# Sums of a weight matrix with ten and seven staging tiles, six column tiles on the first scale, and score tables scaled three steps behind their loads

## The chip, the cores and the metric

The kernel runs on one core of a Trainium2 chip. A core has a matrix engine (PE, TensorE), a vector engine (DVE), an activation engine (ACT), a general engine (POOL, GpSimd) and a queue that issues transfers (SP). Each engine takes its instructions strictly in the order of the program and they meet at semaphores. Working memory is SBUF (128 partitions); PE writes into the eight banks of PSUM.

The metric is the device time of one execution in microseconds. Before the change three runs took 531.81, 538.27 and 540.64 us; the median is 538.27 us.

## The reference, cut to what matters

One encoder block: a combined projection of x (1024 tokens, 1024 features), two groups of attention heads, a gate, an output projection, a residual and a layer norm.

```python
h = x @ W_in                                   # 1024 x 3328 columns
q_a, k_a, v_a, z_a, q_b, k_b, v_b, z_b = split(h)
# group A: 8 heads, 2-D neighbourhood (8 rows x 16 columns of a 16 x 64 grid)
s = einsum(q_a, gathered k_a) * 64**-0.5 + rel_bias       # a table per head and query
y_a = softmax(s) @ gathered v_a
# group B: 8 query heads on 2 key heads, |i - j| <= 128, rotary, a sink logit per head
s = einsum(rotary(q_b), rotary(k_b)) * 64**-0.5           # masked to the band
y_b = softmax(concat(s, sink))[..., :-1] @ v_b
mixed = concat(y_a * silu(z_a), y_b * silu(z_b))
x = layer_norm(2**0.25 * x + mixed @ W_out, gain, bias)
```

## The kernel before, in words

**Numbers.** Most products are computed from 16-bit parts: a matrix is scaled by a power of two and split into a high and a low half, and each product is three matmuls (high by high, high by low, low by high). The value projection uses 32-bit parts instead, so it needs no scale and comes first.

**Scales.** x has one scale, from its largest magnitude. The columns of W_in other than the values' are cut into 21 column tiles of 128 columns (`ORDER`: zb0, z0, zb1, kb, qb0, z1, ...), each in two halves `m` of 512 rows, so there are 42 halves. A scale for the weights comes from sums of magnitudes: `scan_load` (L383) brings a half into a staging tile, `scan` (L388) has ACT sum its magnitudes along each partition. The sums of the first `NG0` column tiles give one scale, those of the others a second one. `chain(i, ...)` (L390 to L403) turns a set of maxima or sums into a scale: a reduction on DVE, a transpose on PE (L394), a second reduction, and some small steps. Chain 0 is x's scale, chain 1 the first weight scale, chain 2 the second.

**The early part** is written out by hand. The value projection (L366) runs in 16 banks, eight for the first half of the tokens and eight for the second. During the second half ACT makes the first sums, and x is loaded a second time (`x2_load`, L411) and split into 16-bit halves (`x16_part`, L421 to L426; on ACT, and on DVE or POOL). ACT copies each bank out (`v_out`, L434), DVE keeps running maxima of the values (`v_max`, L441 and L442). The staging tiles of sums and of x have one tag, `xr`, with four buffers. A weight half for a product is loaded by `w_load` (L146), its high part made on ACT (L157), its low part on POOL in two steps (L162, L163).

After that a planner orders the instructions, by its own estimates: the projections of the first column tiles (`pump_all`, matmuls at L296), the remaining sums, and the values: they are scaled, cast to two 16-bit halves in tiles `vt` with three buffers (L544, L545), stored to a scratch array `vd` (L547) and rearranged from there (L551). The SiLU of the first three gate tiles is taken right from the bank (L262).

**The main loop** is in a hand-written order again. It runs over 128 units (64 of group B, 64 of group A), a unit being 128 queries of a head. In step i: `stage_load` for unit i + `LD`; `stage_qk` (scores, L639 and L640 on PE; the minimum of table plus scores on DVE, L647); `stage_tr` for the unit before (the probabilities are split into halves by ACT, L673, and DVE, L674, and a transposing transfer on SP turns them, L677); `stage_pv` four units at a time (L702); `stage_exp` (L663). Between them `pump_to` puts 48 matmuls of the next column tile, at a set pace. Other work waits in a queue for each engine: `enq` puts an operation in, `pop` takes those whose dependencies were put out in an earlier step, at most so many a step, lowest `prio` first; `need` takes one at once. An operation for SP has a lag of two more steps.

**The score tables** of group A (the bias in a dense layout) are loaded by `stage_load` (L612) into tag `bs` with `BR` = 3 buffers, three tables for eight units, and multiplied in place by a scale on POOL (L614). Before the change that operation has no dependency in its queue and the highest priority, so it is put out in the step of its load.

Of the kernel before, what the change touches and what calls it, by code (L numbers as in the profile page):

```python
# [7 lines left out]
F32 = mybir.dt.float32  # L8
# [11 lines left out]
KT = D // 128  # L20
# [30 lines left out]
def hybrid_block(ctx, tc, xT, x, wt, wv, wo, bias, sink, gain, lbias, cos, sin, bmask, out):  # L51
    nc = tc.nc
# [39 lines left out]
    sg = const.tile([128, 2], F32, name="sg")  # L92
# [48 lines left out]
    NH = 2 * len(ORDER)  # L141
# [176 lines left out]
    with ExitStack() as vctx:  # L318
# [55 lines left out]
        def x_max(half, k):  # L374
            i = 8 * half + k
            nc.vector.tensor_reduce(xm[:, i:i + 1], xh[half, k].bitcast(F32), axis=AXX, op=ALU.max,
                                    apply_absolute_value=True)

        scans = {}

        def scan_load(m):
            scans[m] = vp.tile([128, 512], F32, tag="xr", name="wscan", bufs=4)
            nc.sync.dma_start(scans[m], wt[m // 2, m % 2].rearrange("p k c -> p (k c)"))  # L383

        def scan(m):
# [21 lines left out]

        def x2_load(j):
            if j < len(x2):
                x2raw[j] = vp.tile([128, 512], F32, tag="xr", name="xraw2", bufs=4)  # L410
                nc.sync.dma_start(x2raw[j], xT[x2[j]])  # L411

        def x16_part(j):
# [33 lines left out]
        with tc.manual_schedule():  # L447
            first = load_wv(0, (0, 320, 640)), load_x(0, 0, (0, 256, 512))
            for i in (0, 1, 1):
                next(first[i])  # L450
            interleave(*first)
            interleave(load_wv(1), load_x(0, 1))
            for k in range(KT):
                if k + 2 < KT:
                    interleave(load_wv(k + 2), load_x(0, k + 2))
                if k >= X1AT:
                    interleave(load_x(1, 2 * (k - X1AT)))
                    interleave(load_x(1, 2 * (k - X1AT) + 1))
                    x_max(0, k - X1AT)
                for ps in ([0], [1], [2]) if k == 0 else ([0, 1, 2],):  # L460
                    for a in range(2):
                        for t in range(4):
                            v_mms(banks[2 * t + a], t, a, k, ps)
            nc.sync.dma_start(bm, bmask)
            nc.sync.dma_start(sk, sink)
            for m in range(4):
                scan_load(m)
            for i in range(8):
                v_out(banks[i], i // 2, i % 2)
            for k in range(4, KT):  # L470
                x_max(0, k)
            for k in range(KT):
                x_max(1, k)
            for i in range(8):
                ps = bank(tags[i])
                for k in range(KT):
                    v_mms(ps, 4 + i // 2, i % 2, k)
                v_out(ps, 4 + i // 2, i % 2)
                if i < 2:
                    for m in range(4 * i, 4 * i + 4):  # L480
                        scan(m)
                        if i == 0:
                            scan_load(m + 4)
                        else:
                            x2_load(m - 4)
                if i == 1:
                    chain(0, xm, "ot")
                if 2 <= i < 6:
                    for j in range(4 * (i - 2), 4 * (i - 2) + 4):
                        x16_part(j)  # L490
                        x2_load(j + 4)
                if i == 2:
                    for m in range(4):
                        w_load(m)
                if i == 3:
                    chain(1, wm[0], "ot")
                if i == 4:
                    w_split(0)
                    w_split(1)
                if i == 5:  # L500
                    for nm, src, tag in (("cos", cos, "zc"), ("sin", sin, "zs")):
                        tiles[nm] = zslot(nm, tag)
                        nc.sync.dma_start(tiles[nm], src)
                    nc.vector.tensor_scalar_mul(nsk, sk, -1.0)
                if i > 1:
                    v_max(3)

        for m in range(2 * NG0, 2 * NG0 + 4):
            scan_load(m)
        pump_all(["zb0"])  # L510
        for m in range(2 * NG0, NH):
            scan(m)
            if m + 4 < NH:
                scan_load(m + 4)
# [71 lines left out]
    sns = [ap.tile([128, 388], F32, name=f"sn{i}", bufs=1) for i in range(2)]  # L586
    for t in split:
        nc.gpsimd.memset(t, 0.0)
    LD = 4
    bulk = {"last": None, "step": None}  # L590
    st = {}
    on = {}
# [7 lines left out]
        lo, hi = max(t - 1, 0), min(t + 2, 8)  # L600
        return 128 * (hi - lo), [128] * (hi - lo)

    def stage_load(u):
        g, p, j, t, _ = u
        n, _c = geom(u)
        if g == "a":
            b, half = t
            if half == 0 and b != 2:
                bulk["last"] = clock["step"] + 1
                bt = ap.tile([128, 2, 384], F32, tag="bs", name="bias", bufs=BR)  # L610
                o = 2 * BOFF[b]
                nc.sync.dma_start(bt[:, :, :n], bias[2 * p + j, :, o:o + 2 * n].rearrange("p (h n) -> p h n", h=2))  # L612
                bv = bt[:, :, :n]
                op = enq("pool", lambda: nc.gpsimd.tensor_scalar(bv, bv, rsg, -1.0, op0=ALU.mult, op1=ALU.mult),  # L614
                         prio=0)
                st["bias"] = bt, op
            st[u, "b"] = st["bias"][0][:, half, :n], st["bias"][1]

    def stage_qk(u):
# [27 lines left out]
        nc.vector.tensor_tensor_reduce(sn[:, :n], ps[:, :n], bias_t, sg[:, c:c + 1], init,  # L647
                                       op0=ALU.add, op1=ALU.min, accum_out=nm)
        st[u, "sn"] = sn
# [89 lines left out]
    nc.vector.reciprocal(rsg, sg[:, 1:2])  # L739
# [347 lines left out]
```

## Time and profile before

| what | value |
|---|---|
| runs, median (lowest to highest) | 538.27 us (531.81 to 540.64) |
| the profiled execution | 535.45 us, span 533.7 us |
| PE, DVE, ACT, POOL busy | 87%, 67%, 56%, 41% of the span |
| mean granted PE clock | 0.95 |
| moved by the 16 DMA engines | 89.97 MB, 169 GB/s |

The profile shows one execution. "Busy" counts instructions at work, not waits. A window row gives, for a stretch of time, the busy time of each engine with its instructions in brackets, then the granted clock of PE (1.00 is full speed), the mean busy share of the DMA engines, and GB/s. A wait row names the engine and line that waited, what came last before it could go on, and the total, the count and the longest in us. A timeline row gives start, duration, engine, line, output and input; in square brackets stands the idle time of the engine before it and what ended it. "The chain" is the chain of work that ended last, followed back from the last instruction.

### The profile page before, as it was taken

The numbers are of one execution on the slowest core, as the hardware profiler recorded it, in microseconds if no ns is written. First come the engines' busy times: TensorE is split into PE (matmuls) and PEld (weight loads), VectorE is DVE, ScalarE is ACT, GpSimd is POOL, SyncE is SP. The second block draws the span as 40 slices with busy tenths as digits, with TensorE's granted clock in tenths as the row PEclk, the third lists the DMA queues.
The fourth block names the chain that finished last, engine by engine and source line by source line (L and its number), as shares of the span: only waits on it lengthen the run. The fifth ranks groups of instructions, "written<-read, shape, count | busy, mean of one in ns | idle before, by whom it ended". The sixth has DMA issues, their size and how long they took to land.

```text
span 533.7 us, 9570 instructions
## 1 busy us (share of the span) xinstructions
PE 466.1 (87%) x3243; PEld 302.3 (57%) x3243; DVE 359.5 (67%) x823; ACT 296.5 (56%) x701; POOL 220.9 (41%) x231
## 2 busy tenths in 40 slices
PE   8997697796599999899997839599788999999994
PEld 6996673332244555455554424255444568888883
DVE  5874696537277888889885834476485774929834
ACT  4636256796148787777775734466485764402201
POOL 0003192268634725666214444622346443505331
PEclk9999699989699999999999987799799999999998
DMA  7837557898615676677897878787997898364311
GB/s 252 254 102 215 181 152 281 269 293 286 197 39 102 117 135 137 104 140 118 148 181 187 168 122 184 159 152 160 204 210 127 174 190 248 118 242 133 142 60 60
DMA packets 140737, 89.97 MB, mean 169 GB/s; under 512 B 102032, under 2 KB 118416, under 8 KB 140432
## 3 DMA queue, kind: packets, MB, share of 16 engines
q1 hardware_dynamic: 140544, 89.21, 68.2%
q8 instruction: 25, 0.41, 0.4%
q14 instruction: 24, 0.20, 0.1%
q10 hardware_dynamic: 144, 0.15, 0.1%
HBM read 58.92 MB, written 9.96 MB: 129 GB/s over the span
## 4 chain that ended last, share of the span: by engine, by line
PE 60%; DMA 11%; issue 8%; DVE 7%; ACT 7%; POOL 6%; SPq 1%; POOLq 0%; ACTq 0%; DVEq 0%
PE ps_pj L296 25%; PE ps_s L828 6%; PE ps_t L702 5%; PE ps_t L828 4%; PE ps_pj L828 4%; DMA wscan<-in_wt 4%; DMA bias<-in_bias 3%; PE ps_pj L366 3%; ACT wscan L388 3%; POOL wl L163 3%; PE ps_s L639 3%; PE ps_t L366 3%; PE ps_s L640 2%; PE ps_ot L828 2%; PE ps_s L366 2%
## 5 line engine op out<-in xcount | busy, mean ns | idle before, releaser
L296 PE MATMUL ps_pj<-xf,wh 128*128 128x512 f16 x672 | 207.3, 388 | 8.9 <-ACT wh L157 5.5
L296 PE MATMUL ps_pj<-xf,wl 128*128 128x512 f16 x336 | 130.2, 389 | 29.1 <-POOL wl L163 29.1
L296 PEld LDWEIGHTS <-wh 128*128 128x128 f16 x672 | 64.8, 99 | 73.5 <-issue 9.3
L663 ACT ACTIVATE ps_s<-sn,nm 128x385 f32<-128x385 f32 (+3 forms) x128 | 70.3, 549 | 63.9 <-DVE nm L647 62.8
L674 DVE SCALAR_TENSOR_TENSOR split<-ps_s,split 128x384 f16<-128x384 f32 (+2 forms) x128 | 65.6, 513 | 28.0 <-ACT split L673 27.2
L296 PEld LDWEIGHTS <-wl 128*128 128x128 f16 x336 | 33.5, 100 | 72.5 <-POOL wl L163 34.2
L673 ACT ACTIVATE split<-ps_s 128x384 f16<-128x384 f32 (+2 forms) x128 | 57.5, 449 | 18.4 <-DMA tr<-split 16.6
L162 POOL TENSOR_SCALAR wr<-wr,sc 128x512 f32<-128x512 f32 x42 | 34.1, 812 | 67.6 <-ACT wh L157 50.6
L647 DVE CUSTOM_DVE_ANT_0 sn<-ps_s,bias,sg 128x288 f32<-128x288 f32 (+1 forms) x64 | 36.1, 565 | 37.5 <-PE ps_s L640 30.2
L614 POOL TENSOR_SCALAR bias<-bias,rsg 128x576 f32<-128x576 f32 (+1 forms) x24 | 19.2, 798 | 90.6 <-DMA bias<-in_bias 63.0
L163 POOL TENSOR_TENSOR wl<-wr,wh 128x512 f16<-128x512 f32 x42 | 49.7, 1185 | 3.2
L647 DVE CUSTOM_DVE_ANT_0 sn<-ps_s,bm,nsk 128x384 f32<-128x384 f32 (+1 forms) x64 | 40.8, 638 | 8.9 <-PE ps_s L640 8.3
L639 PE MATMUL ps_s<-ks,qs 128*128 128x384 f16 (+2 forms) x128 | 40.2, 314 | 6.0 <-DVE split L674 4.7
L702 PEld LDWEIGHTS <-tr 128*128 128x128 f16 (+1 forms) x1104 | 38.4, 100 | 7.3 <-DMA tr<-split 5.3
L640 PE MATMUL ps_s<-ks,qs 128*128 128x384 f16 (+2 forms) x128 | 40.2, 314 | 0.0
L157 ACT ACTIVATE wh<-wr,sc 128x512 f16<-128x512 f32 x42 | 29.4, 709 | 11.9 <-PE ps_pj L296 11.9
L388 ACT ACTIVATE wscan<-wscan 128x512 f32<-128x512 f32 x42 | 26.2, 625 | 13.7 <-DMA wscan<-in_wt 13.5
L828 PE MATMUL ps_s<-wo,m 128*128 128x512 f32 (+1 forms) x144 | 32.5, 374 | 0.0
L883 ACT ACTIVATE sd<-mv,eps 128x1 f32<-128x1 f32 x8 | 2.4, 295 | 51.8 <-DVE mv L881 51.8
L423 POOL TENSOR_SCALAR xraw<-xraw,sc 128x512 f32<-128x512 f32 x6 | 5.6, 930 | 58.5 <-ACT xf L421 58.5
L828 PE MATMUL ps_pj<-wo,m 128*128 128x512 f32 (+1 forms) x120 | 28.9, 377 | 0.4 <-POOL m L811 0.4
L220 POOL COPY ks<-ks 64x512 f16<-64x512 f16 x40 | 25.4, 647 | 6.9 <-DVE ks L190 3.5
(148 smaller groups left out, 864.4 us busy)
## 6 DMA issues: line engine op xcount, KB each, us to landing
wscan<-in_wt SPq DMA_DIRECT2D x42, 256.0 KB, 3.6
wr<-in_wt SPq DMA_DIRECT2D x42, 256.0 KB, 3.0
xraw<-in_xT SPq DMA_DIRECT2D x31, 256.0 KB, 3.2
bias<-in_bias SPq DMA_DIRECT2D x16, 288.0 KB, 3.4
wor<-in_wo SPq DMA_DIRECT2D x16, 256.0 KB, 4.6
xr<-in_x SPq DMA_DIRECT2D x8, 512.0 KB, 6.3
out<-xr SPq DMA_DIRECT2D x14, 256.0 KB, 2.1
bias<-in_bias SPq DMA_DIRECT2D x8, 384.0 KB, 3.7
```

Source lines behind the costliest of these rows:

```text
L163: nc.gpsimd.tensor_sub(l, raw, h)
L296: nc.tensor.matmul(ps, a[:, k % 4, :], mv, start=(k == 0 and i == 0), stop=(k == KT - 1 and i == 2))
L366: nc.tensor.matmul(ps[:, :320], lh[t // 4, k][:, ts], rh[k][:, cs], start=(k == 0 and i == 0), stop=(k == KT - 1 and i == 2))
L388: nc.scalar.activation(t, t, AF.Abs, accum_out=wm[g][:, i:i + 1])
L639: nc.tensor.matmul(ps[:, :n], q, sl[0], start=True, stop=False)
L640: nc.tensor.matmul(ps[:, :n], q, sl[1], start=False, stop=True)
L647: nc.vector.tensor_tensor_reduce(sn[:, :n], ps[:, :n], bias_t, sg[:, c:c + 1], init, op0=ALU.add, op1=ALU.min, accum_out=nm)
L663: nc.scalar.activation(pt[:, :m], sn[:, :m], AF.Exp, bias=nm, scale=-1.0, accum_out=sm[:, k:k + 1])
L673: nc.scalar.activation(hl[:, :m, 0, :c], src, AF.Copy, scale=PSCALE)
L674: nc.vector.scalar_tensor_tensor(hl[:, :m, 1, :c], src, PSCALE, hl[:, :m, 0, :c], op0=ALU.mult, op1=ALU.subtract)
L702: nc.tensor.matmul(ps[:, HD * m:HD * m + HD], a, b_, start=(i == 0), stop=(i == len(mms) - 1))
L828: nc.tensor.matmul(ps, lh[:, ts], rh[:, cs], start=(e == EO[0] and i == 0), stop=(e == EO[-1] and i == 2))
```

## The change

It has two parts. In the early part:

- `NG0` goes from 4 to 6: the sums of the first six column tiles (12 halves in place of 8) give the first weight scale, and 30 halves remain for the second.
- The staging tiles of the sums and of the second load of x come from `stage`, which goes round ten buffers: the four of `xr`, three of `wvr` (used for the value weights until then) and three of `vt`; from the 31st on it goes round seven, without `vt`. Ten loads are put out ahead in place of four.
- Chains 0 and 1 stand inside the second and third bank of the second half (after the fifth of their eight parts), in place of after the second and the fourth bank.
- The remaining sums stand, in the program, behind the values' casts and the projections of z0 and zb1; four projections and then chain 2 follow in the order kb, qb0, chain 2, z1. The planner still orders all this.
- Scores of the first B heads are scaled by the first scale twice, so there is a third column in `sg`.

In the main loop: `LD` is 5 in place of 4, `BR` is 4 in place of 3, and the scaling of a table gets a dependency that stands for its load (with SP's lag), so it is put out three steps after it.

```diff
-LTT, LPP, BP, BH, BR, ND, NA, NX, F1 = 1, 5, 2, 7, 3, 1, 1, 6, 0.2
+LTT, LPP, BP, BH, BR, ND, NA, NX, F1 = 1, 5, 2, 7, 4, 1, 1, 6, 0.2
-NG0 = 4
+NG0 = 6
...
-        scans = {}
+        scans, staged = {}, [0]
+
+        def stage(name):
+            tag = ("xr", "xr", "xr", "xr", "wvr", "wvr", "wvr", "vt", "vt", "vt")[staged[0] % (10 if staged[0] < 30 else 7)]
+            staged[0] += 1
+            if tag == "xr":
+                return vp.tile([128, 512], F32, tag="xr", name=name, bufs=4)
+            return vp.tile([128, 640], F32, tag=tag, name=name, bufs=3)[:, :512]
 
         def scan_load(m):
-            scans[m] = vp.tile([128, 512], F32, tag="xr", name="wscan", bufs=4)
+            scans[m] = stage("wscan")
...
-            for m in range(4):
+            for m in range(10):
                 scan_load(m)
...
+            nxt = [10]
+
+            def scan_more(n):
+                for m in n:
+                    scan(m)
+                    if nxt[0] < 2 * NG0:
+                        scan_load(nxt[0])
+                    else:
+                        x2_load(nxt[0] - 2 * NG0)
+                    nxt[0] += 1
+
+            scan_more(range(6))
             for i in range(8):
-                ps = bank(tags[i])
-                for k in range(KT):
-                    v_mms(ps, 4 + i // 2, i % 2, k)
-                v_out(ps, 4 + i // 2, i % 2)
-                if i < 2:
-                    for m in range(4 * i, 4 * i + 4):
-                        scan(m)
...
-                if i == 1:
-                    chain(0, xm, "ot")
...
-                if i == 3:
-                    chain(1, wm[0], "ot")
...
                 if i > 1:
-                    v_max(3)
-
-        for m in range(2 * NG0, 2 * NG0 + 4):
-            scan_load(m)
+                    v_max(2)
+                ps = bank(tags[i])
+                for k in range(KT):
+                    v_mms(ps, 4 + i // 2, i % 2, k)
+                    if i in (1, 2) and k == 4:
+                        chain(i - 1, xm if i == 1 else wm[0], "ot")
+                v_out(ps, 4 + i // 2, i % 2)
+                if i == 0:
+                    scan_more(range(6, 2 * NG0))
+            v_max(16)
+
         pump_all(["zb0"])
-        for m in range(2 * NG0, NH):
-            scan(m)
-            if m + 4 < NH:
-                scan_load(m + 4)
...
+        pump_all(ORDER[1:3])
+        nxt = [2 * NG0]
+        for m in range(2 * NG0, NH):
+            if m < 2 * NG0 + 7:
+                scan_load(m)
+        for m in range(2 * NG0, NH):
+            scan(m)
+            if m + 7 < NH:
+                scan_load(m + 7)
...
-    LD = 4
+    LD = 5
...
-    def stage_load(u):
+    def stage_load(u, i):
...
+                ld = Op("sp", None, [], 1)
+                ld.step = i
                 op = enq("pool", lambda: nc.gpsimd.tensor_scalar(bv, bv, rsg, -1.0, op0=ALU.mult, op1=ALU.mult),
-                         prio=0)
+                         ld, prio=0)
...
-        c = 0 if g == "b" else 1
+        c = min(p, 1) if g == "b" else 2
...
-    pump_all(ORDER[1:NG0 - 1])
+    pump_all(ORDER[3:NG0 - 1])
     chain(2, wm[1], "ot")
...
-    for c in range(2):
-        nc.vector.tensor_scalar(sg[:, c:c + 1], inv[:, c, 0:1], inv[:, 1, 0:1], -0.125 / QSCALE ** 2,
+    for c, (i, j) in enumerate(((0, 0), (0, 1), (1, 1))):
+        nc.vector.tensor_scalar(sg[:, c:c + 1], inv[:, i, 0:1], inv[:, j, 0:1], -0.125 / QSCALE ** 2,
                                 op0=ALU.mult, op1=ALU.mult)
...
-                stage_load(units[i + LD])
+                stage_load(units[i + LD], i)
```

More of the change, by code (lines that the diff above doesn't have):

```diff
@@ L91, in hybrid_block @@
     inv = const.tile([128, 2, 2], F32, name="inv")
-    sg = const.tile([128, 2], F32, name="sg")
+    sg = const.tile([128, 3], F32, name="sg")
     rsg = const.tile([128, 1], F32, name="rsg")
@@ L409, in x2_load @@
             if j < len(x2):
-                x2raw[j] = vp.tile([128, 512], F32, tag="xr", name="xraw2", bufs=4)
+                x2raw[j] = stage("xraw2")
                 nc.sync.dma_start(x2raw[j], xT[x2[j]])
@@ L473, in hybrid_block @@
                 x_max(1, k)
-            for i in range(8):
-                ps = bank(tags[i])
-                for k in range(KT):
-                    v_mms(ps, 4 + i // 2, i % 2, k)
-                v_out(ps, 4 + i // 2, i % 2)
-                if i < 2:
-                    for m in range(4 * i, 4 * i + 4):
-                        scan(m)
-                        if i == 0:
-                            scan_load(m + 4)
-                        else:
-                            x2_load(m - 4)
-                if i == 1:
-                    chain(0, xm, "ot")
+            nxt = [10]
[8 more added lines that the diff above has]
+            scan_more(range(6))
+            for i in range(8):
                 if 2 <= i < 6:
@@ L490, in hybrid_block @@
                         x16_part(j)
-                        x2_load(j + 4)
+                        x2_load(nxt[0] - 2 * NG0)
+                        nxt[0] += 1
                 if i == 2:
@@ L505, in hybrid_block @@
                 if i > 1:
-                    v_max(3)
-        for m in range(2 * NG0, 2 * NG0 + 4):
-            scan_load(m)
+                    v_max(2)
[8 more added lines that the diff above has]
+            v_max(16)
         pump_all(["zb0"])
-        for m in range(2 * NG0, NH):
-            scan(m)
-            if m + 4 < NH:
-                scan_load(m + 4)
         cm = vw.tile([128, 5], F32, name="cm")
@@ L731, in stage_ot @@
                 nc.vector.scalar_tensor_tensor(z, src, z_col(p), z, op0=ALU.mult, op1=ALU.mult)
-    pump_all(ORDER[1:NG0 - 1])
+    pump_all(ORDER[3:NG0 - 1])
     chain(2, wm[1], "ot")
     nc.vector.tensor_scalar(vscb, vsc, inv[:, 1, 1:2], None, op0=ALU.mult)
-    for c in range(2):
-        nc.vector.tensor_scalar(sg[:, c:c + 1], inv[:, c, 0:1], inv[:, 1, 0:1], -0.125 / QSCALE ** 2,
+    for c, (i, j) in enumerate(((0, 0), (0, 1), (1, 1))):
+        nc.vector.tensor_scalar(sg[:, c:c + 1], inv[:, i, 0:1], inv[:, j, 0:1], -0.125 / QSCALE ** 2,
                                 op0=ALU.mult, op1=ALU.mult)
-    nc.vector.reciprocal(rsg, sg[:, 1:2])
+    nc.vector.reciprocal(rsg, sg[:, 2:3])
     pump_all(ORDER[NG0 - 1:NPRO])
```

## The prediction

> **What bounds the kernel now.** The page's busy times come first, then the span cut into its stages, then the waits of each stage.
>
> ```profile
> PE 466.1 (87%) x3243; PEld 302.3 (57%) x3243; DVE 359.5 (67%) x823; ACT 296.5 (56%) x701; POOL 220.9 (41%) x231
> ...
> core 0: us, PE busy (x) PEld busy (x) DVE busy (x) ACT busy (x) POOL busy (x), PEclk, DMA share, GB/s
> 35.40:75.20 39.80, 31.22 (x196) 30.84 (x195) 24.44 (x44) 21.54 (x46) 14.97 (x14) 0.87 0.51 159
> 75.20:161.00 85.80, 68.24 (x301) 29.78 (x301) 48.95 (x90) 47.73 (x108) 43.92 (x47) 0.92 0.70 224
> 161.00:281.30 120.30, 116.70 (x988) 64.89 (x987) 104.38 (x275) 93.50 (x235) 57.24 (x55) 1.00 0.73 134
> 281.30:436.70 155.40, 127.84 (x1095) 72.69 (x1094) 96.47 (x263) 93.55 (x243) 72.41 (x87) 0.92 0.83 170
> 436.70:533.70 97.00, 88.33 (x473) 72.92 (x471) 59.17 (x113) 22.40 (x43) 31.70 (x25) 0.97 0.45 141
> ```
>
> The window rows are stages: second half of the value projection; the first six column tiles (zb0 to z1); the 64 units of group B; the 64 units of group A; the output. PE is the bound in the third: 116.7 of 120.3 us busy at full clock. It isn't in the first, second and fourth, where it idles 8.6, 17.6 and 27.6 us and also loses clock. What it waits for there (from 30 to 140 us, then from 280 to 440 us, then POOL and the load queue):
>
> ```profile
> PE ps_pj L296 <- POOL wl L163: 10.0, 2, 8.1
> PE ps_ot L394 <- DVE gm L392: 8.6, 1, 8.6
> PE ps_pj L296 <- ACT wh L157: 3.6, 2, 2.1
> PE ps_pj L296 <- ACT z L262: 3.4, 3, 2.2
> ...
> PE ps_pj L296 <- POOL wl L163: 18.4, 7, 4.9
> PE ps_t L702 <- DMA tr<-split: 4.3, 6, 1.6
> PE ps_s L639 <- DVE split L674: 3.1, 3, 1.2
> ...
> POOL bias L614 <- DMA bias<-in_bias: 63.0, 15, 10.4
> ...
> SPq L383 <- ACT wscan L388: 30.9, 27, 10.6
> ```
>
> The columns are us in total, times, longest. Two things stand out. Early, PE waits for scales (the chains at L394) and for the weight parts that need them; the sums under those scales are fed by loads that wait for four buffers to come free (30.9 us). Late, PE waits for low weight parts (wl) that POOL makes late, because POOL stands in front of a score table whose load has just been issued.
>
> **The change, part by part.**
>
> *Group A: tables loaded five units ahead, scaled three steps later, one more buffer.* From the chain, the timelines of SP and POOL, and the landing times of the table loads (least, median, most):
>
> ```profile
> 346.70 1.50 PE ps_t L702 x36
> 349.82 1.29 PE ps_pj L296 x6
> 362.33 1.05 PE ps_t L702 x36
> ...
> 352.28 0.57 SPq L612 DMA_DIRECT2D bias<-in_bias  x1
> 356.33 0.90 POOL L614 TENSOR_SCALAR bias<-bias,rsg 128x768 f32<-128x768 f32 x1 [8.21 <-DVE nm L647]
> 357.98 1.16 POOL L163 TENSOR_TENSOR wl<-wr,wh 128x512 f16<-128x512 f32 x1
> ...
> DMA to landing us min/median/max: 3.1/3.5/5.3
> ```
>
> From 346.70 to 362.33 PE never waits: two quads, eight units, 15.63 us, so 1.954 us a unit; 64 units are 125.1 us. The stage takes 155.4, so 30.3 us are stalls and halved clock. The rows at 352 to 358 show the mechanism: the table is asked for at 352.28, the scaling at the head of POOL's queue can't start before 356.33, and wl starts only behind it. (The row names DVE; the landing row says 3.5 us is ordinary for the load.) The next weight load on SP waits for that wl, and the transposes of the probabilities queue behind the load, so one late wl costs two engines.
>
> In the changed kernel the scaling is put into POOL's queue three steps after the load: 3 x 1.95 = 5.9 us, longer than the slowest landing (5.3), and the use is two steps (3.9 us) later. So POOL finds its table there and the 63.0 us of waiting go; what was behind it starts when its own input is ready. All 24 scalings stay, 0.9 us each as in the row above or less, and POOL has room (72.4 of 155.4 us busy). What is late next: the waits for tr and split, 7.4 us together, partly effects of the same blocked queue. I leave 5 us of them; the bounds are 0 and 15. **Term: -25 us, between -30 and -15.** That the 161 to 281 us stage runs PE 97% busy with a like load of ACT and DVE speaks for it. The fourth buffer and the earlier load add 3 KB per partition and no instruction; the loads keep their number and pass one transpose more on SP.
>
> *Twelve sums in the first group, ten staging tiles, chains one bank earlier.* From the chain, the timelines of ACT, DVE and PE, and two windows:
>
> ```profile
> 35.44 7.05 PE ps_pj L366 x48
> ...
> 36.06 0.50 ACT L434 COPY v<-ps_ot 128x320 f32<-128x320 f32 x1
> 39.31 0.63 ACT L388 ACTIVATE wscan<-wscan 128x512 f32<-128x512 f32 x1
> 39.94 0.62 ACT L388 ACTIVATE wscan<-wscan 128x512 f32<-128x512 f32 x1
> ...
> 50.67 0.48 DVE L441 SCALAR_TENSOR_TENSOR vmax<-v,vmax 128x320 f32<-128x320 f32 x1
> 55.13 2.96 DVE L426 SCALAR_TENSOR_TENSOR xf<-xraw,sc,xf 128x512 f16<-128x512 f32 x3
> ...
> 58.21 0.47 PE L394 MATMUL ps_ot<-identf,gm 128*128 128x128 f32 x1 [8.58 <-DVE gm L392]
> ...
> 54.00:58.00 4.00, 0.00 (x0) 0.00 (x0) 3.96 (x5) 1.44 (x3) 1.95 (x2) 0.50 0.86 308
> 60.00:64.00 4.00, 4.00 (x17) 4.00 (x16) 2.68 (x7) 0.00 (x0) 0.00 (x0) 0.50 0.45 144
> ```
>
> A sum is 0.62 us on ACT. Now the transpose of the first weight chain stands on PE after the fourth of eight banks and waits 8.6 us, since its reduction on DVE is queued behind conversions of x. In the changed order it stands inside the third bank, at about 44.9 us (35.4 + 2 banks + five eighths of one, at 7.05/2 = 3.5 us, + a transpose). ACT does six sums from 36.6, a copy, six more: until 44.4; a copy; then the first conversions, from 44.8. DVE has ahead of the reduction two low halves of x (the second when ACT has made its third, 46.8 to 47.5) and two pairs of maxima; three pairs took 50.67 to 55.13, 1.5 us a pair. So the reduction is at about 50.5, the transpose at 50.7: PE waits 5.8 us in place of 8.6, with the rest of its third bank and five more behind it. The clock row: after 8.6 us idle it was 0.50 until 64, with 6 us of work under it, 3 us lost. I keep 2.6 of it. The stage then ends at 50.7 + 1.3 + 5 x 3.5 + 2.6 = 72.1 in place of 75.2. **Term: -3, between 0 and -6.**
>
> The Trainium skill has a rule on this loss: TensorE: Matmul & The Clock Gate, Part 1, The HAM clock gate, says the array drops to half rate after a window of about 3.4 us idle and returns after one busy window of the same length. The trace agrees that 8.6 us idle brings 0.50 and it shows up to three such windows. By the rule 5.8 us idle would cost one or two half-rate windows, 1.7 to 3.4 us: an estimate from that page, against the 2.6 taken.
>
> *The first six tiles on the first scale; the other 30 sums behind them.* From the timelines of ACT, DVE and PE, and the landing times of the value stores:
>
> ```profile
> 105.07 0.71 ACT L544 CAST vt<-v 128x640 f16<-128x640 f32 x1
> 122.10 0.72 ACT L544 CAST vt<-v 128x640 f16<-128x640 f32 x1
> 124.18 0.19 DVE L392 TENSOR_REDUCE gm<-wm 128x1 f32<-128x34 f32 x1 [0.43 <-ACT wscan L388]
> 139.52 0.61 PE L296 MATMUL ps_pj<-xf,wl 128*128 128x512 f16 x1 [8.11 <-POOL wl L163]
> 160.97 0.27 PE L639 MATMUL ps_s<-ks,qs 128*128 128x256 f16 x1
> ...
> DMA to landing us min/median/max: 2.8/4.0/4.4
> ```
>
> Six tiles are 288 matmuls of 1.29/6 = 0.215 us: 62 us, 63.5 with the ten small transposes and the first scores. The stage takes 85.8, so 22.3 us are excess: waits of 17.6 and halved clock. The 8.1 us wait goes: the parts of tiles five and six no longer need the second scale (chain 2, whose reduction ran at 124.18), they need the first, which is there at 52 (50.7 and the chain's small steps). The 3.4 for the SiLU evacuations mostly goes: ten, then seven staging tiles let sums run ahead, so the evacuation doesn't stand behind a sum waiting for its load. Some of the 3.6 us for wh stays.
>
> What is new: ACT's order puts all eight casts of the values ahead of the third tile's second evacuation (zb1's SiLU) and ahead of the last two sums. The casts have three tiles, each free only once its store has landed (4.0 us, the last row), so they go in three rounds: my walk through the order puts the first at 96 us, the rounds at 105 and 111, that evacuation at 113. PE has done kb's first 14 matmuls by 108 and waits for the bank: 5 us. The last two loads on SP stand behind the stores and land at 117; the chain's transpose, at 120 on PE, finds its input. So the excess left is 5, plus 2 for wh, wl and clock: 7. **Term: -15.3, between -22 (no excess) and -4 (the casts take their 17 us from 105 as now and the evacuation comes at 123).**
>
> The extra scale column is one DVE operation, hidden: DVE is busy 49 of 85.8 us there. Same sums, same bytes.
>
> *Unchanged:* group B (PE bound) and the output, 97 us.
>
> **Sum.** 25 + 3 + 15.3 = 43.3. The profiled execution took 535.45 us (span 533.7): 535.45 - 43.3 = 492. The median of the runs, 538.27 (531.81 to 540.64), is 0.5% above it; I don't add that, as it is inside their spread. I predict 491.
>
> **The rivals.**
>
> 1. *Transfers become group A's bound.* A window inside the stage, and the packets of the stage:
>
> ```profile
> 350.00:360.00 10.00, 10.00 (x85) 5.70 (x83) 8.75 (x26) 7.15 (x20) 2.73 (x3) 1.00 0.99 182
> DMA packets 63640, 26.47 MB, mean 169 GB/s; under 512 B 51719, under 2 KB 60935, under 8 KB 63623
> ```
>
> The stage's share of 0.83 over 155.4 us is 129 us of transfer time; at 125 us it would be over 1. Against it: the 350 row has 0.99 at full PE pace. If transfers hold the stage at 0.92, it takes 140: gain 15, 502 us. Chance 0.15. The Trainium skill, DMA: Bandwidth & Descriptors, Specifications, asks for 512 B or more per transfer for full rate; that most packets here are under it agrees with a near-full share at 182 GB/s, and by that rule this rival is the outcome.
>
> 2. *The last two sums and the casts keep the early stage as long as now.* It keeps all but 4 of its excess: 535.45 - 25 - 3 - 4 = 503. Chance 0.13.
>
> 3. *The table change doesn't do what it says*: wl is late for ACT's sake and not for the table's. For it: some scalings' rows name DVE or ACT as releaser. Against it: 63.0 us name the load. Group A unchanged: 517. Chance 0.08.
>
> 4. *Slower: scaled tables come late.* POOL works in order, and the scaling is now placed behind other work, 2 units before use. It decides from a lateness over 3.9 us. Then scores wait on DVE and PE, 24 times; if each costs 2.7 us, 65 us are lost, and with the early gain of 18 and the old stalls gone (-25) the time is 557. Against it: POOL is busy 47% there. Chance 0.04.
>
> **How the numbers follow.** Forecast 491, chance 0.52; all terms at their best, about 478: 0.08. The range takes the forecast, rivals 1 and 2 and most of the good end: 477 to 512. Two per cent (about what measurements of this kernel can tell from no change) would be 527 to 549; only rival 4 and a coincidence of 2 and 3 (528) come near. Faster 0.92, same 0.04, slower 0.04.
>
> **What would show it.** The profile after: POOL's wait for the table near zero and PE's wait for wl after 280 us under 4; group A near 130 us; PE's chain wait near 6 us at 45 to 51; unit 0's scores about 18 to 25 us earlier; a wait of PE for zb1's evacuation at 108 to 113. It is wrong if DMA share in group A is over 0.95 with long tr waits, if the casts run past 120, or if DVE waits for tables.

## The result, and the profile after

The changed kernel takes 491.93 us, the median of four runs (490.97 to 494.27), against 536.57 us of the kernel before in the same comparison: a ratio of 0.920, interval 0.912 to 0.928. The forecast was 491. The profiled execution took 492.28 us, its span is 490.5.

The page's busy times of the changed kernel, and its five stages (start, end, length, busy time of each engine, granted clock of PE, DMA share, GB/s):

```profile
PE 456.6 (93%) x3243; PEld 299.3 (61%) x3243; DVE 360.5 (74%) x824; ACT 295.9 (60%) x701; POOL 225.6 (46%) x231
...
35.40:72.80 37.40, 30.77 (x193) 30.39 (x191) 25.45 (x41) 25.79 (x65) 18.52 (x17) 0.86 0.66 209
72.80:147.40 74.60, 66.56 (x305) 29.85 (x303) 48.92 (x94) 44.09 (x95) 43.77 (x43) 0.98 0.66 213
147.40:267.00 119.60, 116.75 (x1003) 65.25 (x1003) 102.98 (x273) 91.75 (x233) 60.63 (x60) 1.00 0.75 138
267.00:394.50 127.50, 121.27 (x1088) 70.42 (x1084) 97.23 (x265) 94.48 (x243) 70.52 (x84) 0.99 1.03 208
394.50:490.50 96.00, 87.21 (x466) 71.80 (x464) 58.74 (x108) 21.47 (x40) 31.45 (x24) 0.98 0.42 142
```

The same work on PE, in less time: its busy share rises from 87% to 93%. Stage by stage, before and after (the second stage ends about where z1's matmuls end; in the changed kernel the scores of unit 0 stand inside it, at 138.7 us against 161.0 before):

| stage | before | after | difference | forecast |
|---|---|---|---|---|
| value projection, second half | 39.8 | 37.4 | -2.4 | -3 |
| first six column tiles | 85.8 | 74.6 | -11.2 | -15.3 |
| group B | 120.3 | 119.6 | -0.7 | 0 |
| group A | 155.4 | 127.5 | -27.9 | -25 |
| output | 97.0 | 96.0 | -1.0 | 0 |
| sum | | | -43.2 | -43.3 |

The sum is right partly because errors cancel, which is luck: the six tiles gave 4.1 us less than forecast, group A 2.9 more and the output 1.0. The 491 also rests on taking the profiled 535.45 us as the start; from the median of 538.27 the same sum gives 495.

What PE still waits for, from 30 to 140 us and then from 240 to 400 us (total, times, longest):

```profile
PE ps_ot L401 <- DVE gm L399: 6.6, 1, 6.6
PE ps_pj L296 <- ACT z L262: 3.6, 1, 3.6
PE ps_pj L296 <- POOL wl L163: 3.1, 2, 1.8
...
PE ps_pj L296 <- ACT wh L157: 2.4, 1, 2.4
PE ps_pj L296 <- POOL wl L163: 1.7, 2, 1.5
PE ps_t L722 <- DMA tr<-split: 1.6, 3, 0.8
```

The wait of 8.1 us for the second scale is gone, and the 18.4 us for wl in group A are down to 1.7. The two that the forecast named as new or left are there: the first weight chain (6.6), and zb1's evacuation (3.6).

The next rows are from the waits in group A: POOL in the changed kernel, then SP in the kernel before, where it stood with a load of w until POOL had made wl.

```profile
POOL bias L634 <- DMA bias<-in_bias: 27.7, 11, 5.1
```

```profile
SPq L146 <- POOL wl L163: 23.8, 8, 5.0
```

POOL's wait for tables is halved, not gone. The row of SP, 23.8 us before, has no counterpart in the changed kernel: no load of w waits for POOL in group A any more.

### The profile page after: what moved, and what is told of

It reads as the page before. It is cut to its first block, busy times and chain, and to the rows that moved or that the text cites. A ratio compares the mean times of both kernels' runs of the same rounds, so it can differ in the third digit from the quotient of the medians.

```text
span 490.5 us, 9560 instructions
## 1 busy us (share of the span) xinstructions
PE 456.6 (93%) x3243; PEld 299.3 (61%) x3243; DVE 360.5 (74%) x824; ACT 295.9 (60%) x701; POOL 225.6 (46%) x231
## 4 chain that ended last, share of the span: by engine, by line
PE 50%; DMA 14%; DVE 11%; issue 10%; ACT 6%; POOL 6%; SPq 3%; POOLq 0%; ACTq 0%; DVEq 0%
PE ps_pj L296 25%; PE ps_t L722 5%; DMA wscan<-in_wt 4%; PE ps_s L848 4%; PE ps_pj L848 4%; DMA xraw<-in_xT 4%; PE ps_t L848 3%; PE ps_s L659 3%; PE ps_s L660 3%; DMA tr<-split 2%; POOL wl L163 2%; POOL wr L162 2%; PE ps_ot L848 2%; DMA wor<-in_wo 1%; PE ps_ot L742 1%
## 5 line engine op out<-in xcount | busy, mean ns | idle before, releaser
L296 PE MATMUL ps_pj<-xf,wh 128*128 128x512 f16 x672 | 203.8, 382 | 6.4 <-ACT z L262 3.6
L296 PE MATMUL ps_pj<-xf,wl 128*128 128x512 f16 x336 | 127.9, 381 | 5.3 <-POOL wl L163 5.3
L659 PE MATMUL ps_s<-ks,qs 128*128 128x384 f16 (+2 forms) x128 | 39.8, 311 | 4.2 <-DVE split L694 1.9
L660 PE MATMUL ps_s<-ks,qs 128*128 128x384 f16 (+2 forms) x128 | 39.8, 311 | 0.0
L722 PEld LDWEIGHTS <-tr 128*128 128x128 f16 (+1 forms) x1104 | 37.1, 98 | 3.9 <-DMA tr<-split 1.9
L220 POOL COPY ks<-ks 64x512 f16<-64x512 f16 x40 | 28.3, 712 | 7.5 <-DVE ks L190 3.5
```

The costliest lines, as they stand in the source:

```text
L296: nc.tensor.matmul(ps, a[:, k % 4, :], mv, start=(k == 0 and i == 0), stop=(k == KT - 1 and i == 2))
L659: nc.tensor.matmul(ps[:, :n], q, sl[0], start=True, stop=False)
L660: nc.tensor.matmul(ps[:, :n], q, sl[1], start=False, stop=True)
L722: nc.tensor.matmul(ps[:, HD * m:HD * m + HD], a, b_, start=(i == 0), stop=(i == len(mms) - 1))
```

## The experiments

Every ratio is to the kernel before on the same chip in the same comparison; the changed kernel's is 0.920 (0.912 to 0.928). It was not run again beside the experiments, so a difference to it by the ratios carries some 4 us either way. Where the medians in us give another difference, both are given.

### Which part of the table change works

**The table part alone**, on the kernel before, and **the early part alone** (the changed kernel with the table part taken out):

```diff
 # table part alone: kernel before with
-LTT, LPP, BP, BH, BR, ... = 1, 5, 2, 7, 3, ...
+LTT, LPP, BP, BH, BR, ... = 1, 5, 2, 7, 4, ...
...
-    LD = 4
+    LD = 5
...
+                ld = Op("sp", None, [], 1); ld.step = i
-                op = enq("pool", <scale the table>, prio=0)
+                op = enq("pool", <scale the table>, ld, prio=0)
 # early part alone: changed kernel with BR 3, LD 4, and the table enqueued without ld
```

> The kernel before with the table part of the change alone (ring of four tables, loads five steps ahead, scaling three steps behind the load); its early stages are those of before. Theory (the two parts do not touch each other): 267 to 394.5 us of the changed kernel took 127.5 us against 155.4 before, so group A takes 126 to 129 us here too and the early stages what they took before: 535.5 - 28 = 507, range 504 to 511. Rival (the earlier filling of the first score steps is what made room in group A): A keeps 135 us or more and the time is 515 or above.

> The changed kernel with the table part undone (ring of three, loads four steps ahead, scaling with no delay): ten and seven staging tiles and six column tiles on the first scale stay. Theory: the first score step starts near 139 us as in the changed kernel (161 before), group A is back at 150 to 157 us with POOL waiting some 60 us for tables, and the time is 492 + 28 = 520, range 516 to 523; with the run of the table part alone the two gains then add up to the 43 us of the whole. Rival (the parts overlap): the sum of the two gains differs from 43 by more than 5 us.

Measured: the table part 508.85 us, ratio 0.947 (0.942 to 0.953), 28.3 us won; the early part 523.20 us, ratio 0.974 (0.968 to 0.980), 14.0 won. Together 42.3, and the whole change won 42.9 by its ratio: within the scatter the parts add up. The window of group A in each (same columns as the stages):

```profile
284.00:415.30 131.30, 123.80 (x1102) 71.90 (x1100) 97.60 (x268) 94.88 (x246) 71.25 (x85) 0.97 1.01 205
```

```profile
264.40:425.90 161.50, 131.29 (x1105) 74.36 (x1103) 98.65 (x269) 95.39 (x246) 72.56 (x87) 0.92 0.82 166
```

131.3 us with the table part (2.3 over what was expected), 161.5 without it, 4.5 over. The early part's first scores start at 136.2 against 161.0, yet only 14 us reach the end. Most of the rest is no loss: in the kernel before unit 0 stands behind all of z1, in the changed order inside it, so its start moves further than the work does. The scores of the next unit, which stand behind z1 in both, come 15.2 us earlier (the kernel before, then the early part alone):

```profile
162.48 0.33 PE L639 MATMUL ps_s<-ks,qs 128*128 128x384 f16 x1
```

```profile
147.24 0.33 PE L659 MATMUL ps_s<-ks,qs 128*128 128x384 f16 x1
```

**Delay without lead and buffer, and lead and buffer without delay:**

```diff
 # delay alone: changed kernel with BR 3 and LD 4
 # lead and buffer alone: changed kernel with
-                         ld, prio=0)
+                         prio=0)
```

> The changed kernel with the old ring of three tables and loads four steps ahead, the scaling still three steps behind the load (so one step ahead of its use). Theory (the order on POOL is the whole of the gain: the scaling no longer stands in front of the lo parts of w): group A 127 to 132 us, time 491 to 497; a table lands 3.2 to 5.3 us after its issue and three steps are 6, so POOL hardly waits. Rival (the longer lead or the fourth buffer gives the gain): group A 145 us or more, time 509 or above.

> The changed kernel with ring of four and loads five steps ahead, but the scaling handed to POOL with its load, without the delay. Theory (the order on POOL is the cause): POOL again stands 50 us or more in front of tables that have not landed, the lo parts behind come late, group A takes 145 to 157 us and the time is 508 to 522. Rival (lead and buffer): group A stays at 127 to 131 us and the time at 491 to 496.

Measured: the delay alone 497.13 us, ratio 0.925 (0.918 to 0.931); lead and buffer alone 522.13 us, ratio 0.971 (0.964 to 0.978), which is no better than the early part by itself (0.974). Both medians lie 0.1 us above the range of their theory, and some 12 us or more from that of the rival. Group A of the delay alone, and DVE's waits there; then group A of lead and buffer alone, and the waits of POOL, PE and SP there:

```profile
265.90:398.10 132.20, 122.65 (x1089) 71.23 (x1084) 96.78 (x264) 92.69 (x241) 71.04 (x85) 0.97 1.04 199
...
DVE sn L667 <- POOL bias L634: 3.8, 6, 1.0
```

```profile
266.40:424.40 158.00, 129.56 (x1104) 72.69 (x1102) 97.71 (x268) 94.43 (x246) 72.48 (x87) 0.92 0.83 170
...
POOL bias L634 <- DMA bias<-in_bias: 55.6, 15, 8.3
...
PE ps_pj L296 <- POOL wl L163: 14.8, 5, 4.9
...
SPq L146 <- POOL wl L163: 23.5, 7, 4.9
```

So the order on POOL is the cause: the early part alone and the delay alone differ only in the delay, and were measured together at 523.20 and 497.13 us, 26 us apart. A table loaded a unit earlier but scaled in the step of its load still has POOL stand in front of the transfer for 55.6 us, and the chain wl, next load of w, transposes behind it is back. What lead and buffer add behind the delay is small: by the traces group A takes 132.2 us without them and 127.5 with them, and the scaled table is just too late now and then without them (DVE's 3.8 us; none in the changed kernel). That is rival 4 in small, with its mechanism but not its price. The ratios, 0.925 and 0.920, do not tell the two kernels apart.

### Are transfers the bound of group A now?

```diff
+                bt2 = ap.tile([128, 2, 384], F32, tag="bs2", name="bias2", bufs=2)
+                nc.sync.dma_start(bt2[:, :, :n], <the same table>)
```

> The changed kernel in which each of the 24 score tables is loaded a second time, into two buffers that nobody reads: 7.9 MB more beside the 26.5 MB that group A moves (16 tables of 128x576 and 8 of 128x768 words). Theory (transfers do not set group A's length, although their share reads 1.03): group A stays under 134 us and the time under 499. Rival (transfers are the bound of group A now): a share of 1.03 over 127.5 us is 131 us of transfer time, and 7.9 of 26.5 MB more of it is 39 us: group A 150 to 166 us, the time 515 to 531. Between the two, 499 to 515: the transfers are near the bound and come in its way now and then.

Measured: 505.97 us, ratio 0.938 (0.936 to 0.940), about 10 us more than the changed kernel by the ratios, 14 by the medians. Between the two theories, as the third case said. Group A of this run, with ACT's waits there, and ACT's in the changed kernel:

```profile
268.10:408.30 140.20, 124.41 (x1085) 70.98 (x1081) 96.61 (x264) 92.59 (x241) 70.22 (x84) 0.98 1.10 242
...
ACT split L695 <- DMA tr<-split: 24.2, 17, 4.5
```

```profile
ACT split L693 <- DMA tr<-split: 6.0, 14, 1.4
```

12.7 us more in group A for 7.9 MB, where 39 were to come if transfers set its length. The rate went from 208 to 242 GB/s and the share from 1.03 to 1.10, so a share of 1.03 was not the most that could be reached. But the transposes now wait. The run doesn't tell bandwidth from SP's time: each added load also takes SP about half a microsecond, 24 of them 11 us, in front of the transposes.

### The early part: staging tiles, six tiles, and an order of reads

```diff
 # four staging tiles: in stage()
-            tag = ("xr", ..., "vt")[staged[0] % (10 if staged[0] < 30 else 7)]
+            tag = "xr"
 # four tiles on the first scale
-NG0 = 6
+NG0 = 4                    # 8 loads ahead, 8 sums in the first group
 # the same, window reads last: the loop "dma_start(vwin[b], ...)" is moved behind the remaining sums
```

> The changed kernel with four staging tiles, as before, in place of ten and seven; the twelve sums in the first group and everything else stay. Theory (the staging tiles are what lets the twelve sums come in time): only four loads stand ready when ACT begins the sums at 36.6 us, the other eight come at the pace of the transfers, some 1.3 us each, so the first weight chain ends 3 to 6 us later than 51 and the last 30 sums run late as before: time 497 to 505. Rival (the six tiles on the first scale are the whole of the early gain): chain 1 within 2 us of 51 and time 490 to 495.

> The changed kernel with four column tiles on the first scale, as before, instead of six: 8 sums under the first scale and 34 under the second; the ten and seven staging tiles and the place of the chains stay. Theory (the six tiles are what takes the wait for the second scale away): the fifth tile's low weight part needs the second scale, whose transpose ran at 124.8 us, so it comes at about 128 and PE waits 4 to 9 us there: time 496 to 501. Rival (the staging tiles alone bring the second scale early enough): no such wait over 2 us, time 490 to 494.

> The run with four column tiles on the first scale, with the four reads of the value windows (3.7 MB) issued behind the load for the last sum instead of ahead of it. In that run this load, issued at 117.3, took 12.9 us and the second scale's transpose ran at 131.3. Theory (the load stood behind the window reads): it lands in 3 to 6 us, the transpose runs at 121 to 125, PE's waits for the second scale and its weight parts fall from 18.2 to 6 to 11 us and the time is 499 to 505; what is then left against the changed kernel is what six tiles on the first scale are worth by themselves. Rival (the order of the reads does not matter, the load lands late for another reason): 507 to 512.

Measured: four staging tiles 502.24 us, ratio 0.932 (0.925 to 0.938); four tiles first 510.07 us, ratio 0.946 (0.944 to 0.948); with the reads moved 505.62 us, ratio 0.938 (0.931 to 0.944). From the timelines of the run with four tiles first (SP, ACT, PE, and the landing times of L390 from 90 to 130 us):

```profile
114.63 2.57 SPq L559 DMA_DIRECT2D vwin<-vd  x4
117.30 0.53 SPq L390 DMA_DIRECT2D wscan<-in_wt  x1
...
130.34 0.63 ACT L395 ACTIVATE wscan<-wscan 128x512 f32<-128x512 f32 x1 [11.54 <-DMA wscan<-in_wt]
...
131.34 0.47 PE L401 MATMUL ps_ot<-identf,gm 128*128 128x128 f32 x1 [13.17 <-DVE gm L399]
...
DMA to landing us min/median/max: 3.0/5.2/12.9
```

One load behind 3.7 MB of window reads took 12.9 us and held the second scale. With the reads behind it, PE's row is:

```profile
122.09 0.48 PE L401 MATMUL ps_ot<-identf,gm 128*128 128x128 f32 x1 [5.78 <-DVE gm L399]
129.51 1.89 PE L296 MATMUL ps_pj<-xf,wh 128*128 128x512 f16 x4 [6.95 <-ACT wh L157]
136.31 0.61 PE L296 MATMUL ps_pj<-xf,wl 128*128 128x512 f16 x1 [4.92 <-POOL wl L163]
```

The scale comes 9 us earlier, as expected, but PE's waits fall only from 21.1 us (18.2 without the last, for wl) to 17.6 and not to 6 to 11: behind the scale stand wh on ACT and wl on POOL, which no projection can start without, and both expectations left them too small. Counted from here, six tiles on the first scale are worth 0.938 - 0.920, some 9 us by the ratios and 14 by the medians; the staging tiles 0.932 - 0.920, some 6 and 10, with an interval that overlaps that of the changed kernel. The whole early part won 14, so whether the two gains add or are partly the same is left open. The time with four staging tiles lies in the range of its theory, but where the staging tiles act is not where the expectation put it. Below, PE's and SP's rows with four of them, then SP's in the changed kernel:

```profile
52.96 0.47 PE L401 MATMUL ps_ot<-identf,gm 128*128 128x128 f32 x1 [10.39 <-DVE gm L399]
...
42.19 10.13 SPq L418 DMA_DIRECT2D xraw<-in_xT  x8
```

```profile
38.02 12.36 SPq L418 DMA_DIRECT2D xraw<-in_xT  x14
```

The twelve sums end only a microsecond later (44.8 us against 43.8). But the second load of x, in the same ring, is put out from 42.2 instead of 38.0, its conversions stand on DVE ahead of the chain's reduction, and the transpose waits 10.4 us in place of 6.6. It runs only 1.9 us later, at 52.96 instead of 51.03; the rest of the longer wait is PE's earlier arrival. The last sum does not run late either (115.2 us, 119.5 in the changed kernel), as the expectation had it. The larger part comes later: PE waits for evacuations of gate tiles for 7.7 us in place of 3.6, and the second unit's scores stand at 155.9 instead of 148.5. What holds these is not taken apart here.

### The two waits that are left: the first chain, and zb1's evacuation

```diff
 # chain first
-                if i > 1:
+                if i > 2:
                     v_max(2)            # the other variant: v_max(3)
 # stores of the cast values from another queue
-            nc.sync.dma_start(vd[...], vt[...])
+            nc.gpsimd.dma_start(vd[...], vt[...])     # the other variant, on chain first with v_max(3): nc.scalar
```

> The changed kernel with the first two pairs of maxima of the values (3 us on DVE, 46.7 to 50.8) behind the reduction of the first weight chain instead of ahead of it. Theory (those two pairs are what the chain's 6.6 us wait is made of, and the wait brings the halved clock): PE's wait for the reduction falls to 1.5 to 3.6 us, the clock of the second half of the value projection rises from 0.86 to 0.95 or more, that stage ends 4 to 6 us earlier and the time is 486 to 489. Rival (the sums and casts behind set the first six tiles, whatever comes ahead): the stage ends earlier but the first score step stays near 138.7 and the time at 490 to 493.

> The run with the first weight chain ahead of the maxima, with three pairs of maxima at each later bank instead of two, so that fewer are left for the end, where PE waited 1.8 us for them. Theory (each early wait is worth its size): chain wait stays near 2.5, the wait for the maxima goes, the time is 0.5 to 2 us under that run: ratio to before 0.904 to 0.909. Rival (PE is held 4 us at the third tile's evacuation in any case, which takes up what came earlier): ratio 0.908 to 0.913.

Measured: chain first 489.71 us, ratio 0.909 (0.907 to 0.911), its interval below that of the changed kernel (0.912 to 0.928); with three pairs 491.60 us, ratio 0.909 (0.903 to 0.916), no gain over it. The first lies between its theory (486 to 489 us) and its rival (490 to 493). The chain in the changed kernel (the last sum on ACT, then DVE, then PE), and its transpose in chain first:

```profile
43.08 0.66 ACT L395 ACTIVATE wscan<-wscan 128x512 f32<-128x512 f32 x1
...
46.68 1.44 DVE L448 SCALAR_TENSOR_TENSOR vmax<-v,vmax 128x320 f32<-128x320 f32 x1
...
50.82 0.16 DVE L399 TENSOR_REDUCE gm<-wm 128x1 f32<-128x12 f32 x1
...
51.03 0.47 PE L401 MATMUL ps_ot<-identf,gm 128*128 128x128 f32 x1 [6.63 <-DVE gm L399]
```

```profile
45.59 0.32 PE L401 MATMUL ps_ot<-identf,gm 128*128 128x128 f32 x1 [2.48 <-DVE gm L399]
```

The sums end at 43.8; two pairs of maxima, 46.68 to 50.8, were the wait. Without them ahead, the wait is 2.5 and the clock of this stage 1.00 in place of 0.86. The first column tile starts at 64.7 us instead of 72.8 (4.1 from the wait, some 2.7 from the clock, 1.3 because PE came to the chain earlier in this run), and the first scores at 132.6 instead of 138.7. But this profile is of the fastest of four runs, 485.92 us. With three pairs (profiled at 491.98 us) the wait is the same 2.5, the clock halves behind it (the last section), and the first scores come at 138.3, hardly earlier than in the changed kernel. So taking the maxima away from the chain takes 4.1 us of waiting away for certain; what reaches the end is 6 us by the ratios and 2.2 by the medians, and that chain first beats the changed kernel is likely but not settled.

> The changed kernel with the eight stores of the cast values issued from POOL's queue instead of SP's, where three of them stood 3.5 us behind a load of w that waited for its buffer. Theory (the cast rounds hold back the third tile's second evacuation, and what holds the casts is the stores' place in SP's queue): the second round of casts starts near 104 us (107.7), that evacuation near 111 (114.5), PE's wait of 3.6 us for it falls under 1, and the time is 487 to 490. Rival (the landing itself, some 4 us a round, holds the casts): the evacuation stays at 113 to 115 and the time at 491 to 493.

> The same with the eight stores of the cast values issued from ACT's own queue. On SP they stood behind loads of w; on POOL they began at 103.1, behind POOL's weight parts, and cost POOL 0.8 us each, and no time was won. Theory (the stores hold the casts, the casts the evacuation): the stores begin near 98, the third tile's second evacuation stands no longer behind them, PE's wait of 4.0 us for it falls under 1.5, ratio 0.899 to 0.905. Rival (ACT now waits for DVE's half of each cast tile ahead of its stores, and its sums and weight parts come later by as much): ratio 0.906 to 0.915.

Measured: stores on POOL 495.97 us, ratio 0.920 (0.917 to 0.924), no gain; stores on ACT 490.44 us, ratio 0.910 (0.905 to 0.915), no gain either. The second is built on chain first with three pairs of maxima, and is to be compared with that (491.60, 0.909). In the changed kernel the casts and the evacuation behind them ran so (ACT, then PE):

```profile
98.32 1.97 ACT L552 CAST vt<-v 128x640 f16<-128x640 f32 x3
...
107.74 2.23 ACT L552 CAST vt<-v 128x640 f16<-128x640 f32 x3 [3.60 <-DMA vd<-vt]
111.76 0.73 ACT L552 CAST vt<-v 128x640 f16<-128x640 f32 x1 [1.16 <-POOL vb L554]
...
114.51 0.67 ACT L262 ACTIVATE z<-ps_pj,inv 128x512 f32<-128x512 f32 x1
...
115.23 1.01 PE L296 MATMUL ps_pj<-xf,wh 128*128 128x512 f16 x2 [3.62 <-ACT z L262]
```

The stores in the two runs (line of stores, first and last start):

```profile
L555 POOL DMA_DIRECT2D vd<-vt x8: 813/822/976, 103.1 to 120.9; - x8
```

```profile
L555 ACTq DMA_DIRECT2D vd<-vt x8: 366/366/388, 98.8 to 111.7; - x8
```

In both, that evacuation comes some 5 us earlier (at 109.1 and 109.3 us, 114.5 and 114.2 without the edit) and PE's wait for it is gone, as the theory said, but the time does not follow. On POOL the gain is eaten on the way: waits for wl (4.5 us against 3.1), q's parts (1.9 against 0.9) and a gate tile on DVE (2.4, none before), beside POOL's 6.6 us of store issues; the second unit's scores come at 148.9, as in the changed kernel (148.5). With the stores on ACT the first scores do come earlier than in the kernel it is built on (that kernel first, then with the stores on ACT):

```profile
138.26 0.28 PE L659 MATMUL ps_s<-ks,qs 128*128 128x256 f16 x1 [0.98 <-DVE qs L192]
```

```profile
133.92 0.39 PE L659 MATMUL ps_s<-ks,qs 128*128 128x256 f16 x1 [2.50 <-DVE qs L192]
```

Of these 4.3 us the spans of the two profiles show 0.9 (490.2 and 489.3); where the rest goes is not shown. The stores did hold the evacuation, then, but a theory that took the length of that one wait as its price was wrong here twice.

## Why the prediction was right or wrong, point by point

- **What bounds the kernel** (idle PE in stages one, two and four): right. PE does the same work and the stages shrink by what it idled and lost in clock.
- **Group A, -25: right in mechanism, 27.9 in size.** The step that was off is "POOL finds its table there and the 63.0 us of waiting go". 27.7 remain. Three steps were no 5.9 us between load and scaling: SP runs behind its steps, waiting for the transposes' inputs, and the scaling starts mostly 3.4 to 5.4 us after the load is issued, still at the landing. One such pair, on SP and POOL:

```profile
324.34 0.57 SPq L630 DMA_DIRECT2D bias<-in_bias  x1
...
327.92 0.75 POOL L634 TENSOR_SCALAR bias<-bias,rsg 128x576 f32<-128x576 f32 x1 [4.67 <-DMA bias<-in_bias]
```

  The wait costs little, since what stood behind it needlessly, wl, now stands ahead. What is left in the stage is not what was forecast either: of the 5 us for tr and split PE waits 1.9 between 267 and 394.5 us, but also 2.4 for wh and 1.5 for wl. It comes out shorter than forecast because the 125.1 us, taken from eight units in which PE never waited, were too long as a floor: PE is busy 121.3 of the 127.5.
- **Value projection, -3: right**, 2.4. The transpose at 51.03 (50.7), the wait 6.6 (5.8), the order of events on DVE as walked through. That the time fits so well is luck in part: the conversions of x were done 0.8 us earlier than forecast, and the two pairs of maxima took 4.1 us, not 3. The halved clock ran from 46.8 to 57.0 us: six microseconds of work under it, 3 lost, 2.6 taken. The estimate from the Trainium skill's TensorE: Matmul & The Clock Gate, Part 1 (one or two half-rate windows, 1.7 to 3.4 us) agrees with these 3 us. The half rate itself lasted 10.2 us, 4.2 of them idle.
- **First six tiles, -15.3: sign and mechanism right, 4.1 us too much.** The mis-sized term is "2 for wh, wl and clock". 74.6 less 63.5 of work is an excess of 11.1: 3.6 for the evacuation (5 forecast; rounds of casts at 98, 107.7 and 111.8, walked through as 96, 105, 111), and 7.5 of the rest: two waits for wl (3.1), q's parts and a raw tile (1.2), and half clock from 115 to 118.4 (1.7), with 1.5 spread out. The runs above took such a wait away twice, without a shorter time to show for it.
- **Rival 1, transfers as group A's bound: fell.** Half of its sign came, a share of 1.03 (over 0.95); the long tr waits did not. Doubling the tables shows how near it was: 7.9 MB more cost 12.7 us in this stage. The prediction read the Trainium skill, DMA: Bandwidth & Descriptors, Specifications (512 B or more per transfer for full rate), as a rule by which this rival comes true. The trace does not bear this reading out: 51836 of the 63757 packets of the stage are under 512 B, and 207 GB/s go beside a PE that is 95% busy:

```profile
DMA packets 63757, 26.50 MB, mean 207 GB/s; under 512 B 51836, under 2 KB 61052, under 8 KB 63740
```

- **Rival 2** (sums and casts keep the early stage long): fell; zb1's evacuation at 114.5, the last sum at 119.5. Something like it comes true with four tiles first, where the last load stands behind the window reads and the first scores come at 164.2, not before 161.0.
- **Rival 3** (wl late for ACT's sake): fell with the run of lead and buffer alone, where wl is late with POOL's waits for tables and nothing else is changed.
- **Rival 4** (scaled tables late): no wait of DVE for a table in the changed kernel; 3.8 us with three buffers.

## What to carry to other kernels

An operation that waits for a transfer belongs in an in-order queue where the transfer has landed, not where it is issued: the place in the queue was worth about 26 us here, more buffers and an earlier load without it nothing. Ask of every wait what stands behind it: a wait with nothing urgent behind (27.7 us of POOL) cost little here, and a few microseconds of maxima ahead of a chain cost a wait and a stretch of half clock behind it. A wait that is taken away need not come back as time, so price it by the run and not by its length.

## What the hardware showed that was not expected

The same idle stretch of PE, 2.48 us, halved the clock in two profiles and not in a third. Windows around it, first of chain first, then of the same with three pairs of maxima, to which the run with stores on ACT is alike (the two numbers behind the busy times are clock and DMA share):

```profile
46.00:48.00 2.00, 2.00 (x16) 2.00 (x15) 1.22 (x8) 0.73 (x2) 1.92 (x3) 1.00 0.74 217
```

```profile
46.00:48.00 2.00, 2.00 (x9) 2.00 (x10) 1.27 (x8) 0.00 (x0) 1.92 (x3) 0.50 0.76 245
```

In the second the clock is at half from 46 to about 49.4 us. So a wait of 2.5 us can bring some 3.4 us of half clock; that the runs of chain first spread from 485.92 to 491.20 us may come from this, which no run here shows. And a DMA share of 1.03 left room: 1.10 at 242 GB/s was reached with more bytes.
